# Layer 1 of a two-layer diffusion backbone: query products and the expert blocks computed ahead in plain float32, from weights that are not split

## The chip, the cores and the metric

One Trainium2 chip; the kernel runs on one of its cores. The metric is the device time of one execution in microseconds, lower is better. A core has TensorE (PE; its weight loads are listed as PEld), VectorE (DVE), ScalarE (ACT), GpSimd (POOL) and SyncE (SP), which here issues nearly all DMAs. The kernel keeps its tiles in SBUF on 128 partitions, and its matmuls write to a ring of eight PSUM tiles.

## The reference

Two layers, each a mixer (conv, attention, Hyena and SSD groups between an input and an output projection) and then a PEER expert layer. All is float32. The mixer is the same before and after; the change is in the expert layer:

```python
def peer(h, wq, sub_keys, u_tab, v_tab):          # h: tokens x 1024
    q = (hb @ wq).reshape(128, 8, 2, 128)          # 8 heads, two half queries
    s = einsum('thpk,hpnk->thpn', q, sub_keys)     # scores against 128 keys per half
    v1, i1 = top_k(s[:, :, 0], 16); v2, i2 = top_k(s[:, :, 1], 16)
    cv, ci = top_k(v1[..., :, None] + v2[..., None, :], 16)   # best 16 of the pairs
    e = i1[ci // 16] * 128 + i2[ci % 16]           # expert numbers out of 16,384
    g = softmax(cv)
    act = gelu(einsum('td,ted->te', hb, u_tab[e]))
    return einsum('te,ted->td', g * act, v_tab[e])
```

In layer 1 only the 256 latent tokens go through it (two tiles of 128 tokens); layer 0 has 512 (256 latent, 256 context).

## The kernel before

**Dense experts.** For all but one tile of layer 0 the experts are not gathered. The 16,384 experts are 128 blocks of 128; for each block the kernel computes all activations (`u_stage`: eight k-slices of the block against the token columns `hT`, gelu), multiplies them by a dense gate matrix that is zero except at the chosen experts (`weights`), and multiplies the result with the block of v (`values`, `accum`, into PSUM tiles `ov`).

**Split products.** A float32 product is made of three float32r matmuls (`mm3`, lines 141 to 143). Both operands are first split (`split`, lines 136 to 138): ACT casts to `hi` (line 137), and another engine subtracts to get `lo` (line 138). For the query weights (`load_w`, tile `w_raw`) and the blocks computed ahead that engine is POOL; in the main loop, and for the last four blocks computed ahead, it is DVE.

**Stages of layer 1's expert layer**, in the order of the program:

1. `to_hT` (line 781) transposes the tokens, applies the modulation and splits the result into `hT[0]`, `hT[1]`.
2. For q = 0 to 15, `wq(q)` loads 128 columns of the query weights, splits them and multiplies (tile `pq`, copied to `qs`); `top(q-1)` scores against the keys (tile `ss`, line 1050, two tiles of tokens, plain float32) and takes the best 16 on DVE (lines 1058 to 1062). After every fourth q, `pairs` (lines 1071 to 1135) combines four halves into expert numbers and gates, nearly all on DVE.
3. `u_stage` for blocks 0 to 11, then (`UE`) for 12 to 17.
4. `slots` transposes the routing (`tr`, `slT`); `hots` and `gates` (lines 1182 to 1218) build the gate matrix: for each of 16 groups of 16 tokens DVE makes `Ah`, `Al` (line 1206) and `B_` (line 1209), PE makes 32 float16 matmuls into `G`, ACT copies them to `stg`, and SP writes 1 MB to DRAM (`Gd`). After each group one `u_stage` is issued (blocks 18 to 33); four more follow the last.
5. The main loop runs `u_stage(38)` to `u_stage(127)`, each with the gating and the v-product of a block 38 earlier. It needs the gate matrix read back (`gt`), so the first `ov` matmul of the layer comes after the last `Gd` write.

The tiles of activations (`act`) are 38 (`UA` + `UB`), hence 38 blocks ahead. `u_raw` has three buffers in layer 1 (`URB`), `w_raw` three, and the `hi` and `lo` of a block three each (of the query weights three, `WB`). All loads of `u_raw` are issued after the last load of query weights, on SP's queue, in order with the `Gd` writes. A planner orders the instructions of each engine from its own estimate of their durations; within an engine that order is then fixed.

Of the kernel before, what the change touches and what calls it, by code (L numbers as in the profile page):

```python
# [20 lines left out]
D = 1024  # L21
# [23 lines left out]
NE = 2  # L45
WHB = (4, 5)
WB = 3
FL = 6
FM = 11
LF = 200  # L50
NF = 2
HB = 3
GTB = (4, 4)
GRB = (3, 2)
UEV = (0, 0)
# [28 lines left out]
def tile_hybrid_diffusion(ctx: ExitStack, tc: tile.TileContext, I: dict, out: bass.AP):  # L84
    nc = tc.nc
    V, S, G, T = nc.vector, nc.scalar, nc.gpsimd, nc.tensor
    uid = [0]

    def pool(name, bufs=1, stack=ctx, **k):
        uid[0] += 1  # L90
        if "space" not in k:
            k["reuse_waits"] = "tile"
        return stack.enter_context(tc.tile_pool(name=f"{name}{uid[0]}", bufs=bufs, **k))
# [3 lines left out]
    def mk(p, shape, dt=F32, tag=None, name=None, **k):  # L97
        uid[0] += 1
        n = f"{name or tag}_{uid[0]}"
        if tag in SCR:  # L100
            k["bufs"] = SCR[tag]
        return p.tile(shape, dt, tag=tag or n, name=n, **k)
# [17 lines left out]
    def bank(name="pb"):  # L120
        return mk(ps, [128, 512], F32, tag="b", name=name)
# [12 lines left out]
    late = {}  # L134

    def split(src, hi, lo, eng=None):
        S.copy(hi, src)  # L137
        late["V" if eng in (None, V) else "G"] = (eng or V).tensor_tensor(lo, src, hi.bitcast(F32), ALU.subtract)  # L138

    def mm3(o, lh, ll, rh, rl, first, last):  # L140
        T.matmul(o, lh, rh, start=first, stop=False)  # L141
        T.matmul(o, lh, rl, start=False, stop=False)  # L142
        return T.matmul(o, ll, rh, start=False, stop=last)  # L143
# [97 lines left out]
    def load_w(wp, src, n=128, eng=None, bufs=2, rb=3):  # L241
        raw = mk(wp, [128, 8, 128], tag="w_raw", bufs=rb)
        late["D"] = nc.sync.dma_start(raw[:, :, :n], src)
        hi = mk(wp, [128, 8, 128], F32R, tag="w_hi", bufs=bufs)
        lo = mk(wp, [128, 8, 128], F32R, tag="w_lo", bufs=bufs)
        split(raw[:, :, :n], hi[:, :, :n], lo[:, :, :n], eng or G)
        return hi, lo
# [54 lines left out]
    def ln_mod(l, which, mod, m0):  # L302

        lt = mk(smp, [128, 4, 8], tag="lnT", bufs=2)
        nc.sync.dma_start(lt, I["lnT"][l])
        cc = mk(smp, [128, 2, 8, 2], tag="lnc", bufs=2)
        sc, sh = mod[:, m0 + 8:m0 + 16, :], mod[:, m0:m0 + 8, :]
        for j in range(2):
            V.tensor_tensor(cc[:, j], sc, lt[:, 2 * which + j, :, None].to_broadcast([128, 8, 2]), ALU.mult)
        V.tensor_tensor(cc[:, 1], cc[:, 1], sh, ALU.add)  # L310
        return cc
# [466 lines left out]
        run(ssd(), attention(), hyena(), conf_norm(), more)  # L778
        mp_s.close()

    def to_hT(tiles, xsrc, cc, hT, p, back=None, hb=2):

        for t in tiles:
            s = t // 2
            for q in range(2):
                b = bank("xT")
                for j in range(4):
                    k = 4 * q + j
                    T.transpose(b[:, j * 128:(j + 1) * 128], xsrc(t)[:, k * 128:(k + 1) * 128], ident)
                h = mk(p, [128, 4, 128], tag="h", bufs=hb)  # L790
                for j in range(4):
                    k = 4 * q + j
                    sc, sh = cc[:, 0, k, s:s + 1], cc[:, 1, k, s:s + 1]
                    if j % 2:
                        S.activation(h[:, j, :], b[:, j * 128:(j + 1) * 128], AF.Identity, bias=sh, scale=sc)
                    else:
                        V.tensor_scalar(h[:, j, :], b[:, j * 128:(j + 1) * 128], sc, sh, op0=ALU.mult, op1=ALU.add)
                sl = slice(t * 128, t * 128 + 128)
                split(h, hT[0][:, 4 * q:4 * q + 4, sl], hT[1][:, 4 * q:4 * q + 4, sl])
                if back and t in back:  # L800
                    b = bank("hb")
                    for j in range(4):
                        T.transpose(b[:, j * 128:(j + 1) * 128], h[:, j, :], ident)
                    S.copy(back[t][:, q * 512:q * 512 + 512], b)
# [28 lines left out]
    def fill_to(l, c):  # L833
        while done[-1] < (l, c) and next(fill, None):
            pass
# [7 lines left out]
    for l in range(2):  # L843
        NS = 2 if l == 0 else 1
        NT = 256 * NS
        NTL = 2 * NS
        GT = [3] if l == 0 else []
        DT = [t for t in range(NTL) if t not in GT]
        ND = 128 * len(DT)
        modT = modTs[l]  # L850
        if l == 0:
            hT = [mk(hp, [128, 8, 512], F32R, tag=f"hT{j}") for j in range(2)]

        order = ExitStack()
        with ExitStack() as mx:
            wp = pool("wp", bufs=2, stack=mx)
# [14 lines left out]
            else:  # L871
                with ExitStack() as hs_:
# [40 lines left out]
                    for k in range(0, 8, 2):  # L913
                        for s in range(2):
                            sl = slice(s * 256, s * 256 + 256)
                            h = mk(hmp, [128, 2, 256], tag="h2")
# [29 lines left out]
            if l == 0:  # L946
                xp_s = ExitStack()
                x_n = mk(pool("xp", stack=xp_s, side="right"), [128, 4, D], name="x_n")
# [18 lines left out]
            for m in range(8):  # L967
                wt = load_w(wp, I["w_out"][l, m], eng=V, bufs=WLB[l], rb=WRB[l])
                b = bank("po")
# [3 lines left out]
                for s in range(NS):  # L973
                    sl = slice(s * 256, s * 256 + 256)
# [11 lines left out]
            lnc = ln_mod(l, 0, modT, 24)  # L986
# [12 lines left out]
        hT = [mk(hp, [128, 8, 512], F32R, tag=f"hT{j}") for j in range(2)]  # L999
        if GT:  # L1000
            h2n = mk(rk, [128, D], name="h2n")
# [1 line left out]
        rings = [(up, UA[l])]  # L1003
        gsl = {}

        def u_stage(bl, eng=None):
            raw = mk(up, [128, 8, 128], tag="u_raw", bufs=URB[l])
            with tc.issue_after(late["D"].ins):
                nc.sync.dma_start(raw, I["uT"][l, bl])
            hi = mk(up, [128, 8, 128], F32R, tag="u_hi", bufs=2 + l)  # L1010
            lo = mk(up, [128, 8, 128], F32R, tag="u_lo", bufs=2 + l)
            split(raw, hi, lo, eng)
            b = bank("au")
            for k in range(8):
                mm3(b[:, :ND], hi[:, k, :], lo[:, k, :], hT[0][:, k, :ND], hT[1][:, k, :ND], k == 0, k == 7)
            p, n = rings[0] if bl % (UA[l] + UB[l]) < UA[l] else rings[1]
            a = mk(p, [128, ND], tag="act", bufs=n)
            S.activation(a, b[:, :ND], AF.Gelu_apprx_tanh)
            acts[bl] = a

        with ExitStack() as rt:
            rp = pool("rp", stack=rt)
            sl4 = mk(rp, [128, NTL, 4, 8, 16], name="sl4")
            dec = mk(rp, [128, 3, 16], F16, name="dec")
            nc.sync.dma_start(dec, I["dec"])
            with ExitStack() as wqs:
                wp = pool("wq", bufs=2, stack=wqs)
                rp2 = pool("rp2", bufs=1, stack=wqs)
                if l:
                    prep.clear()  # L1030
                    prep.update(raw=(wp, 2))
                to_hT(range(NTL), lambda t: x_n[:, t, :], lnc, hT, rp2, {3: h2n} if GT else None, HB)
                keys = mk(rp2, [128, 16, 128], tag="keys", bufs=1)
                nc.sync.dma_start(keys, I["keys"][l])
                n8 = 2 * NTL
                vs, ixs, sq = {}, {}, {}

                def wq(q):
                    hi, lo = load_w(wp, I["wq"][l, q], bufs=WB)
                    b = bank("pq")  # L1040
                    for k in range(8):
                        mm3(b[:, :NT], hi[:, k, :], lo[:, k, :], hT[0][:, k, :NT], hT[1][:, k, :NT], k == 0, k == 7)
                    sq[q] = mk(rp2, [128, NT], tag="qs", bufs=2)
                    S.copy(sq[q], b[:, :NT])

# [91 lines left out]
                for q in range(17):  # L1137
# [6 lines left out]
                    if q:  # L1144
                        top(q - 1)
                        if q % 4 == 0:
                            pairs(q // 4 - 1)
                    if done[-1] < (1, (FL, 11)[l]):
                        next(fill)
                fill_to(1, (FL, 11)[l])  # L1150
                ahead = iter(range(min(UA[l] + UB[l], 128)))
                for bl in range(UA[l]):
                    u_stage(next(ahead), G)
            xp_s.close()
            if l == 0:
                fwp_s.close()
# [62 lines left out]

            cur = hots(slots(DT[0]))  # L1220
            for _ in range(UE[l]):
                u_stage(next(ahead), V if UEV[l] else G)
            for i, t in enumerate(DT):
                for tb in range(8):
                    gates(t, tb, *cur)
                    if i + 1 < len(DT):
                        if tb == 2:
                            nxt = slots(DT[i + 1])
                        elif tb == 7:
                            nxt = hots(nxt)  # L1230
                    if tb % 8 in UM[l]:
                        for bl in ahead:
                            u_stage(bl, G)
                            break
                cur = nxt
            for bl in ahead:
                u_stage(bl)


        UBl = UA[l] + UB[l]  # L1240
        with ExitStack() as vst:
# [85 lines left out]
            if l == 0:  # L1327
                lnc = ln_mod(l, 1, modTs[1], 0)
# [16 lines left out]
            for st in range(UBl, last + UBl):  # L1345
                if st < 128:
                    u_stage(st)
                bl = st - UBl
# [17 lines left out]
            x_n = mk(pool("xp", stack=xp_s, side="right"), [128, len(DT), D], name="x_n")  # L1366
# [8 lines left out]
            if l == 0:  # L1375
                hT = [mk(hp, [128, 8, 512], F32R, tag=f"hT{j}") for j in range(2)]
# [152 lines left out]
```

## Time and profile before

| | |
|---|---|
| median of 3 runs | 2943.63 us (2938.61 to 2950.10) |
| profiled execution, time | 2948.22 us |
| profiled execution, span of the core | 2946.4 us |
| mean granted TensorE clock | 0.957 of full speed |
| busy share of the span | PE 90%, PEld 78%, DVE 71%, ACT 40%, POOL 26% |
| share of the chain that ended last | PE 46%, DVE 20%, DMA 14%, issue 12%, POOL 5%, ACT 3% |

Times in the rows are counted from the start of the span. Layer 1's expert layer begins at about 2045. A matmul's duration in the trace includes its way through the array, and matmuls overlap; what one costs in a stream is the distance of two starts. Where rows say x8, eight instructions are merged into one row.

### The profile page before, as it was taken

Reading aid. Unit: us, or ns where it says so; the run is one execution under the profiler, and the core shown is the slowest. Engines: PE = TensorE matmul, PEld = TensorE weight load, DVE = VectorE, ACT = ScalarE, POOL = GpSimd, SP = SyncE. Lnnn points to the kernel's source line nnn. Section 1 sums busy time; section 2 is a strip of 40 time slices with the busy share of each in tenths; the row PEclk is TensorE's granted clock in tenths of the full one; section 3 lists DMA queues with packets and bytes.
Section 4 is the critical chain, followed back from the end, with each engine's and each line's share of the span. In section 5 each row is a group of like instructions: output and inputs, shape, how many; then the busy total and the mean of one; then the engine's idle time right before and its main releaser. Section 6 shows DMA issues by size and latency. Waiting matters only on the chain.

```text
span 2946.4 us, 41926 instructions
## 1 busy us (share of the span) xinstructions
PE 2656.8 (90%) x15646; PEld 2286.7 (78%) x15646; DVE 2099.5 (71%) x4255; ACT 1164.1 (40%) x1810; POOL 778.3 (26%) x505
## 2 busy tenths in 40 slices
PE   6798879688899999999999998788778999999997
PEld 3674557478899988888888987656777999999986
DVE  4956448989687778777767646964999865555556
ACT  2333533235433333333333334334345544444443
POOL 2333013134224444444334103321564100000000
PEclk9899989889899999999999999998888999999999
DMA  7122434336899999988889645325336986666656
GB/s 255 57 90 94 150 122 137 112 117 245 286 334 311 326 321 321 319 307 302 305 308 308 200 129 179 119 82 183 115 116 231 319 272 202 217 209 210 200 181 197
DMA packets 241840, 625.08 MB, mean 212 GB/s; under 512 B 22424, under 2 KB 104794, under 8 KB 236004
## 3 DMA queue, kind: packets, MB, share of 16 engines
q1 hardware_dynamic: 201156, 475.05, 48.6%
q0 software_dynamic: 40480, 147.36, 14.1%
q8 instruction: 122, 2.00, 0.3%
q14 instruction: 82, 0.67, 0.1%
HBM read 573.04 MB, written 49.30 MB: 211 GB/s over the span
## 4 chain that ended last, share of the span: by engine, by line
PE 46%; DVE 20%; DMA 14%; issue 12%; POOL 5%; ACT 3%; SPq 0%; POOLq 0%; DVEq 0%; ACTq 0%
DMA grow<-in_vg_dram,eu 8%; PE ov L142 6%; PE ov L141 6%; PE ov L143 5%; POOL grow L1311 5%; PE au L141 4%; PE au L143 4%; PE au L142 4%; DVE yT L365 2%; PE pj L141 1%; PE pj L142 1%; PE pj L143 1%; DMA wa_raw<-in_w_ada_dram 1%; DVE accg L1324 1%; DVE e L1067 1%
## 5 line engine op out<-in xcount | busy, mean ns | idle before, releaser
L143 PE MATMUL au<-hT,u_lo 128*128 128x384 f32 (+1 forms) x2048 | 642.0, 314 | 12.6 <-POOL u_lo L138 10.0
L141 PE MATMUL au<-hT,u_hi 128*128 128x384 f32 (+1 forms) x2048 | 645.4, 315 | 6.4 <-ACT u_hi L137 3.4
L142 PE MATMUL au<-hT,u_hi 128*128 128x384 f32 (+1 forms) x2048 | 641.5, 313 | 0.0
L142 PE MATMUL ov<-v_lo,wh 128*128 128x512 f32 x1280 | 505.2, 395 | 28.2 <-DVE v_lo L138 27.8
L143 PE MATMUL ov<-v_hi,wl 128*128 128x512 f32 x1280 | 500.1, 391 | 0.0
L141 PE MATMUL ov<-v_hi,wh 128*128 128x512 f32 x1280 | 462.9, 393 | 5.9 <-ACT wh L137 5.6
L137 ACT CAST u_hi<-u_raw 128x1024 fp32r<-128x1024 f32 x256 | 268.7, 1050 | 496.1 <-PE au L142 319.8
L141 PEld LDWEIGHTS au<-hT,u_hi 128*128 128x128 f32 x2048 | 394.1, 192 | 15.3 <-ACT u_hi L137 4.2
L143 PEld LDWEIGHTS au<-hT,u_lo 128*128 128x128 f32 x2048 | 393.2, 192 | 15.6 <-POOL u_lo L138 10.9
L142 PEld LDWEIGHTS au<-hT,u_hi 128*128 128x128 f32 x2048 | 394.1, 192 | 7.7
L138 DVE TENSOR_TENSOR v_lo<-v_raw,v_hi 128x1024 fp32r<-128x1024 f32 x255 | 312.8, 1227 | 79.4 <-ACT v_hi L137 79.1
L138 DVE TENSOR_TENSOR u_lo<-u_raw,u_hi 128x1024 fp32r<-128x1024 f32 x198 | 242.0, 1222 | 148.1 <-ACT u_hi L137 148.1
L137 ACT CAST v_hi<-v_raw 128x1024 fp32r<-128x1024 f32 x256 | 268.3, 1048 | 143.2 <-DMA v_raw<-in_v_dram 109.5
L142 PEld LDWEIGHTS ov<-v_lo,wh 128*128 128x128 f32 x1280 | 241.8, 189 | 84.2 <-DVE v_lo L138 40.9
L137 ACT CAST wh<-act 128x384 fp32r<-128x384 f32 (+1 forms) x256 | 116.9, 459 | 431.1 <-PE ov L142 419.7
L141 PEld LDWEIGHTS ov<-v_hi,wh 128*128 128x128 f32 x1280 | 242.0, 190 | 51.4 <-ACT wh L137 5.9
L143 PEld LDWEIGHTS ov<-v_hi,wl 128*128 128x128 f32 x1280 | 241.5, 189 | 49.7
L138 POOL TENSOR_TENSOR w_lo<-w_raw,w_hi 128x1024 fp32r<-128x1024 f32 (+1 forms) x72 | 176.9, 2466 | 251.5 <-ACT w_hi L137 219.6
L138 POOL TENSOR_TENSOR u_lo<-u_raw,u_hi 128x1024 fp32r<-128x1024 f32 x58 | 171.4, 2961 | 257.3 <-ACT u_hi L137 250.8
L1311 POOL DMA_INDIRECT grow<-in_vg_dram,eu x128 | 179.0, 1398 | 221.5 <-DVE accg L1324 167.2
L1311 POOL DMA_INDIRECT grow<-in_ug_dram,eu x128 | 160.6, 1255 | 262.8 <-DVE grow L1315 232.2
L1324 DVE SCALAR_TENSOR_TENSOR accg<-grow,ag,accg 128x1024 f32<-128x1024 f32 x127 | 162.8, 1282 | 75.8 <-DMA grow<-in_vg_dram,eu 75.1
(832 smaller groups left out, 4324.9 us busy)
## 6 DMA issues: line engine op xcount, KB each, us to landing
u_raw<-in_uT_dram SPq DMA_DIRECT2D x256, 512.0 KB
v_raw<-in_v_dram SPq DMA_DIRECT2D x256, 512.0 KB
Gd<-stg SPq DMA_DIRECT2D x40, 1024.0 KB
gt<-Gd SPq DMA_DIRECT2D x80, 512.0 KB
wa_raw<-in_w_ada_dram SPq DMA_DIRECT2D x76, 512.0 KB
w_raw<-in_w_in_t_dram SPq DMA_DIRECT2D x44, 512.0 KB
w_raw<-in_wq_dram SPq DMA_DIRECT2D x32, 512.0 KB
w_raw<-in_w_ada_dram SPq DMA_DIRECT2D x20, 512.0 KB
```

The source lines that it names most:

```text
L137: S.copy(hi, src)
L138: late["V" if eng in (None, V) else "G"] = (eng or V).tensor_tensor(lo, src, hi.bitcast(F32), ALU.subtract)
L141: T.matmul(o, lh, rh, start=first, stop=False)
L142: T.matmul(o, lh, rl, start=False, stop=False)
L143: return T.matmul(o, ll, rh, start=False, stop=last)
L365: V.scalar_tensor_tensor(uc, upad[:, m, :, j:j + 256], wj, uc, op0=ALU.mult, op1=ALU.add)
L1067: V.tensor_tensor(x[:, :, :, 0:w], x[:, :, :, 0:w], x[:, :, :, w:2 * w], ALU.add)
L1311: nc.gpsimd.indirect_dma_start(out=r, out_offset=None, in_=I[tab], in_offset=bass.IndirectOffsetOnAxis(ap=eu[:, i:i + 1], axis=0))
L1324: V.scalar_tensor_tensor(accg, r, ag[:, i:i + 1], accg, op0=ALU.mult, op1=ALU.add)
```

## The change

Three pairs of switches, all off for layer 0 and on for layer 1. `to_hT` writes its result in float32 into a new tile `h32` and does not split it; the split into `hT` for the main loop is issued inside `wq(1)`. `wq` loads the query weights into five buffers (`PRB`) and multiplies them unsplit with `h32`, one plain float32 product per k-slice. `u_stage` does the same for the 38 blocks computed ahead. The main loop is as before.

```diff
+PW = (0, 1)
+PU = (0, 1)
+PRB = (4, 5)
...
-    def to_hT(tiles, xsrc, cc, hT, p, back=None, hb=2):
+    def to_hT(tiles, xsrc, cc, hT, p, back=None, hb=2, h32=None):
...
-                h = mk(p, [128, 4, 128], tag="h", bufs=hb)
+                h = h32(t)[:, 4 * q:4 * q + 4, :] if h32 else mk(p, [128, 4, 128], tag="h", bufs=hb)
...
-                split(h, hT[0][:, 4 * q:4 * q + 4, sl], hT[1][:, 4 * q:4 * q + 4, sl])
+                if not h32:
+                    split(h, hT[0][:, 4 * q:4 * q + 4, sl], hT[1][:, 4 * q:4 * q + 4, sl])
...
-        def u_stage(bl, eng=None):
+        def u_stage(bl, eng=None, plain=False):
             raw = mk(up, [128, 8, 128], tag="u_raw", bufs=URB[l])
             with tc.issue_after(late["D"].ins):
                 nc.sync.dma_start(raw, I["uT"][l, bl])
+            if plain:
+                b = bank("au")
+                for k in range(8):
+                    T.matmul(b[:, :ND], raw[:, k, :], h32[0][:, k, :ND], start=k == 0, stop=k == 7)
+                return act_of(bl, b)
...
                 def wq(q):
-                    hi, lo = load_w(wp, I["wq"][l, q], bufs=WB)
                     b = bank("pq")
-                    for k in range(8):
-                        mm3(b[:, :NT], hi[:, k, :], lo[:, k, :], hT[0][:, k, :NT], hT[1][:, k, :NT], k == 0, k == 7)
+                    if PW[l]:
+                        raw = mk(wp, [128, 8, 128], tag="w_raw", bufs=PRB[l])
+                        late["D"] = nc.sync.dma_start(raw, I["wq"][l, q])
+                        o = 0
+                        for h in h32:
+                            n = h.shape[-1]
+                            for k in range(8):
+                                T.matmul(b[:, o:o + n], raw[:, k, :], h[:, k, :], start=k == 0, stop=k == 7)
+                            o += n
+                        if q == 1:
+                            for i in range(0, 8, 2):
+                                split(h32[0][:, i:i + 2, :], hT[0][:, i:i + 2, :ND], hT[1][:, i:i + 2, :ND])
...
-                    u_stage(next(ahead), G)
+                    u_stage(next(ahead), G, PU[l])
...
-                u_stage(next(ahead), V if UEV[l] else G)
+                u_stage(next(ahead), V if UEV[l] else G, PU[l])
...
-                            u_stage(bl, G)
+                            u_stage(bl, G, PU[l])
...
-                u_stage(bl)
+                u_stage(bl, None, PU[l])
```

## Rows read from the trace of the kernel before

**Rows 1.** Busy by stretch: length, PE, PEld, DVE, ACT, POOL, clock, DMA, GB/s.

```profile
2323.00:2900.00 577.00, 575.87 (x3535) 518.15 (x3535) 353.03 (x572) 278.90 (x416) 6.79 (x9) 1.00 0.69 222
2052.00:2323.00 271.00, 218.62 (x1904) 212.88 (x1904) 240.50 (x628) 126.72 (x215) 125.32 (x48) 0.89 0.53 177
2063.00:2192.00 129.00, 97.94 (x713) 95.38 (x712) 124.31 (x543) 54.61 (x87) 69.24 (x28) 0.87 0.35 112
2222.00:2307.00 85.00, 73.67 (x826) 71.33 (x824) 81.02 (x49) 50.37 (x92) 35.91 (x13) 0.96 0.76 261
```

**Rows 2.** POOL's groups, 2040 to 2310.

```profile
L138 POOL TENSOR_TENSOR u_lo<-u_raw,u_hi 128x1024 fp32r<-128x1024 f32 x34 | 91.6, 2702 | 89.9 <-ACT u_hi L137 85.9 <-PE au L142 2.2 <-PE G L1216 1.8
L138 POOL TENSOR_TENSOR w_lo<-w_raw,w_hi 128x1024 fp32r<-128x1024 f32 x16 | 39.3, 2464 | 31.8 <-ACT w_hi L137 31.7
```

**Rows 3.** DVE in order of time: start, duration, line.

```profile
2076.93 2.53 DVE L1083 TENSOR_TENSOR cand<-v 128x8 f32<-128x8 f32 x3
...
2113.33 2.11 DVE L1133 TENSOR_SCALAR rb<-rb 128x64 f32<-128x64 f32 x1
...
2172.06 0.20 DVE L1133 TENSOR_SCALAR rb<-rb 128x64 f32<-128x64 f32 x1
...
2182.72 2.67 DVE L1067 TENSOR_TENSOR e<-e 128x128 f16<-128x128 f16 x2
...
2226.48 1.21 DVE L1206 TENSOR_TENSOR Ah<-o,o 128x2048 f16<-128x2048 f16 x1
```

**Rows 4.** DVE's costliest groups, 2192 to 2306.

```profile
L1206 DVE TENSOR_TENSOR Al<-o,o 128x2048 f16<-128x2048 f16 x16 | 30.4, 1902 | 0.0
L1206 DVE TENSOR_TENSOR Ah<-o,o 128x2048 f16<-128x2048 f16 x16 | 29.4, 1843 | 4.7 <-PE G L1215 4.7
```

**Rows 5.** PE in order of time, at three places.

```profile
2602.00 0.28 PE L141 MATMUL au<-hT,u_hi 128*128 128x256 f32 x1
2602.12 0.28 PE L142 MATMUL au<-hT,u_hi 128*128 128x256 f32 x1
...
86.04 1.89 PE L238 MATMUL kf<-h4a,dft 128*128 128x256 f32 x8
...
2115.24 0.61 PE L1050 MATMUL ss<-keys,qs 128*128 128x128 f32 x4
```

**Rows 6.** Plain float32 products: count, least/median/longest duration, first and last start.

```profile
L238 PE MATMUL kf<-h4a,dft x32: 377/379/379, 86.0 to 179.1; 128*128 128x256 f32 x32
...
L1050 PE MATMUL ss<-keys,qs x64: 272/275/583, 2062.6 to 2133.3; 128*128 128x128 f32 x64
```

**Rows 7.** Layer 1's tokens, queries and blocks ahead: tiles xT, qs, au.

```profile
L795 ACT ACTIVATE h<-xT,lnc x8: 451/457/476, 2047.4 to 2055.6; 128x128 f32<-128x128 f32 x8
...
L1044 ACT COPY qs<-pq x16: 359/367/392, 2062.2 to 2132.4; 128x256 f32<-128x256 f32 x16
...
L141 PE MATMUL au<-hT,u_hi x312: 278/283/563, 2133.3 to 2322.6; 128*128 128x256 f32 x156
```

**Rows 8.** The gate stage and the first v-product: tiles G, stg, ov.

```profile
L1215 PE MATMUL G<-Ah,B__3321_18911 x16: 218/218/233, 2221.5 to 2223.2; 128*128 128x128 f16 x16
...
L1217 ACT ACTIVATE stg<-G x64: 587/602/677, 2219.7 to 2306.6; 128x512 f32<-128x512 f32 x64
...
L141 PE MATMUL ov<-v_hi,wh x512: 388/389/497, 2323.4 to 2930.7; 128*128 128x512 f32 x171
```

**Rows 9.** PE's longest waits, 2052 to 2320: total, times, longest.

```profile
PE ss L1050 <- ACT qs L1044: 16.9, 5, 8.3
PE G L1215 <- DVE Ah L1206: 12.1, 2, 7.5
```

**Rows 10.** A block's load: issue on SP, and its cast on ACT.

```profile
2139.94 3.24 SPq L1009 DMA_DIRECT2D u_raw<-in_uT_dram  x2
...
2143.89 1.04 ACT L137 CAST u_hi<-u_raw 128x1024 fp32r<-128x1024 f32 x1
```

**Rows 11.** The page's group of a split on DVE.

```profile
L138 DVE TENSOR_TENSOR u_lo<-u_raw,u_hi 128x1024 fp32r<-128x1024 f32 x198 | 242.0, 1222 | 148.1 <-ACT u_hi L137 148.1
```

More of the change, by code (lines that the diff above doesn't have):

```diff
@@ L1015, in u_stage, with act_of @@
                 mm3(b[:, :ND], hi[:, k, :], lo[:, k, :], hT[0][:, k, :ND], hT[1][:, k, :ND], k == 0, k == 7)
+            act_of(bl, b)
+        def act_of(bl, b):
             p, n = rings[0] if bl % (UA[l] + UB[l]) < UA[l] else rings[1]
@@ L1024, in tile_hybrid_diffusion @@
             dec = mk(rp, [128, 3, 16], F16, name="dec")
+            h32 = []
+            if PW[l]:
+                h32.append(mk(rp, [128, 8, ND], name="h32"))
             nc.sync.dma_start(dec, I["dec"])
@@ L1031, in tile_hybrid_diffusion, with cols32 @@
                     prep.update(raw=(wp, 2))
-                to_hT(range(NTL), lambda t: x_n[:, t, :], lnc, hT, rp2, {3: h2n} if GT else None, HB)
+                if PW[l] and GT:
+                    h32.append(mk(rp2, [128, 8, 128], name="h32g"))
+                def cols32(t):
+                    return h32[1] if t in GT else h32[0][:, :, t * 128:(t + 1) * 128]
+                to_hT(range(NTL), lambda t: x_n[:, t, :], lnc, hT, rp2, {3: h2n} if GT else None, HB, cols32 if PW[l] else None)
                 keys = mk(rp2, [128, 16, 128], tag="keys", bufs=1)
@@ L1038, in wq @@
                 def wq(q):
-                    hi, lo = load_w(wp, I["wq"][l, q], bufs=WB)
                     b = bank("pq")
-                    for k in range(8):
-                        mm3(b[:, :NT], hi[:, k, :], lo[:, k, :], hT[0][:, k, :NT], hT[1][:, k, :NT], k == 0, k == 7)
+                    if PW[l]:
+                        raw = mk(wp, [128, 8, 128], tag="w_raw", bufs=PRB[l])
[9 more added lines that the diff above has]
+                                split(h32[0][:, i:i + 2, :], hT[0][:, i:i + 2, :ND], hT[1][:, i:i + 2, :ND])
+                    else:
+                        hi, lo = load_w(wp, I["wq"][l, q], bufs=WB)
+                        for k in range(8):
+                            mm3(b[:, :NT], hi[:, k, :], lo[:, k, :], hT[0][:, k, :NT], hT[1][:, k, :NT], k == 0, k == 7)
                     sq[q] = mk(rp2, [128, NT], tag="qs", bufs=2)
```

## The prediction, made before the changed kernel was run

> **What bounds the kernel now.** I read busy time by stretch first. In the main loop, 2323 to 2900, PE is busy for 575.87 of 577 us [rows 1]: that stretch is PE's work and the change does not touch it. So the change is worth what it moves the first v-product, at 2323.4 [rows 8]. Ahead of that, from 2052, PE is busy for 218.62 of 271 us at a granted clock of 0.89, while DVE is busy for 240.50 and, while the experts are chosen, for 124.31 of 129 [rows 1]. The chain of waits, read in order of time, agrees: between the first scores and the last gates it is made almost wholly of DVE pieces.
>
> Then I asked why DVE is so busy. Read in order of time, the same operation on the same shape takes 2.11 us in one place and 0.20 in another [rows 3], and each long one lies beside one of POOL's subtractions, of which there are 16 of 2.46 us and 34 of 2.70 [rows 2]. From 2063 to 2192 I count 23 such stretched rows, the first and the last of them in [rows 3], about 1.8 us over their like: 41 us. In the gate stage `Al` and `Ah` take 1.90 and 1.84 us on average against 1.21 undisturbed [rows 3, 4]: 16 x 0.69 + 16 x 0.63 = 21 us, and other operations of that stage wait too.
>
> PE's longest waits in this part are for scores and gates that hang on DVE [rows 9].
>
> **The change part by part.**
>
> *POOL's 50 subtractions go,* and with them 54 casts of ACT and the four subtractions of the last blocks ahead, which DVE did. Nothing of POOL's is left in this part. Value for DVE: 41 us while the experts are chosen and at least 21 at the gates. Its ends: nothing, if the stretched operations wait for something else, and all of it.
>
> *Each product of three float32r matmuls becomes a plain float32 one.* Three float32r matmuls of 256 columns cost 3 x 0.12 us (starts 2602.00 and 2602.12 [rows 5]), so 8 k-slices cost 2.88. For plain float32 the row is `kf`: eight instructions of 256 columns in 1.89, of which the last's own way through is 0.38 [rows 5, 6], so (1.89 - 0.38) / 7 = 0.216 each. The trap is the count. Layer 1's scores are 16 x 2 = 32 products in the code, and the trace has 64 [rows 6]; `kf` is 16 products in the code, and the trace has 32. A plain product is two instructions, 0.43 us, and a block is 16 x 0.216 = 3.46 us. So PE gets slower: 16 query products and 38 blocks, 54 x (3.46 - 2.88) = 31 us more work. The switch that saves the splits costs TensorE.
>
> The Trainium skill has two sentences on this. "FP8 and Floating Point Precision", section "TensorE Precision Notes", says that true FP32 takes four passes through the array; "Perfetto Trace Analysis", section "Engine Utilization", halves the output rate for FP32_LOW_HIGH. The trace sides with the four: each instruction takes somewhat under twice a float32r one's time, and there are two. By the second alone a block would be 1.73 us; that is rival 3.
>
> *`to_hT` no longer splits; the split is inside `wq(1)`.* The tokens are ready at about 2051 instead of 2055.6 [rows 7], as four subtractions of DVE no longer stand between them. The same four, with four casts, come after `pq(1)`: some 0.6 us each on DVE, half of a block's 1.22 [rows 11], 2.5 in all. They lie in DVE's wait for the first scores, since PE now needs 3.46 + 0.4 us a query (four score instructions, (0.61 - 0.28) / 3 = 0.11 each [rows 5, 6]) and DVE some 2.4; without that cover they cost 2.5 us of DVE. The first result on DVE moves little, to about 2062.
>
> *Five buffers of query weights, three of blocks.* A load now holds its buffer until PE has multiplied. A block's load was issued at 2139.94 and its cast began at 2143.89 [rows 10], so about 4 us; with three buffers a block can follow every (4 + 0.5 + 3.46) / 3 = 2.7 us, less than the 3.46 that PE takes. SP's queue holds the `Gd` writes and the loads in order; in the gate stage a round moves 1 MB + 0.5 MB. At PE's pace, below, that is 1.57 MB in 5.3 us, 296 GB/s, against 261 at a DMA share of 0.76 [rows 1], so a share of 0.86. I charge a few us for loads that come late there; bounds 0 and, if the DMA share can't go above 0.76, 16 x 0.7 = 11 us.
>
> *What is late next: PE.* Its work from the first query product to the first v-product, at full clock: queries 16 x 3.46 = 55; scores 64 x 0.11 = 7; 38 blocks x 3.46 = 131; 16 groups of 32 gate matmuls, sixteen of them 1.7 us apart [rows 8], so 1.85 a group, 30; block 38 of the main loop 2.9; transposes 1. Together 227 us; before it was 196, which took 271 with 23 lost to a lower clock (196 / 0.89 is the 219 of busy time) and 52 waiting.
>
> DVE no longer limits it. From 2062 it has 83 us of choosing left (124 - 41) and 2.5 of splits, so the routing is ready near 2150, where it was 2192; PE, queries and scores behind it at 2051 + 62 + some 5, is then in blocks 0 to 17 (18 x 3.46 = 62 us, to about 2180), and the first gates can be built under them. In the gate stage PE needs 1.85 + 3.46 = 5.3 us a group, DVE 3 x 1.21 = 3.6 [rows 3], ACT 4 x 0.6 and a gelu. The pace before was (2306.6 - 2219.7) / 15.75 = 5.5, so the stage hardly gains; the gain is that it starts earlier.
>
> The sum: first v-product at 2051 + 227 = 2278 with no waiting and full clock, a gain of 45 at most. I take 17 us of the former 75 as staying: some 4 for a slow first product, 5 for heads of queue while DVE sets the pace of the scores, 4 for late loads, 4 for clock after gaps. Gain 2323 - 2295 = 28 us. From the profiled execution's 2948.2 that is 2920; its median is 4.6 below that execution, so 2943.6 - 28 = 2916.
>
> **The rivals.**
>
> 1. *No change.* The gaps of PE stay because they come from order (blocks behind the last query product, the transposes behind DVE), not from the stretched operations. If 44 of the 75 us stay, the 31 us of extra work eat the gain. For it: order on PE is fixed, and 16.9 us of waits hang on ACT's copies. Against it: those copies wait for DVE. Time about 2942.
>
> 2. *Slower: PE is the bound and its clock does not rise.* PE waits as before, because each query now takes 3.9 us, and scores reach DVE later by what DVE saves; the extra work then runs at 0.89 beside the same 52 us of waiting: 227 / 0.89 + 52 = 307 us against 271, so +36 at the worst and about +15 if a third of the waits goes: 2959. It decides once more than 271 - 255 = 16 us of waiting stays at that clock. For it: the clock is 0.87 while the experts are chosen. Against: it is 1.00 where PE is never idle, and 0.96 in the gate stage [rows 1], and PE will be idle less.
>
> 3. *A plain product costs one instruction's time.* Then a block takes 1.73, PE's work falls to 227 - 54 x 1.73 = 134, and DVE sets the pace: routing at 2148, first gates copied 15 us later, 15.75 groups at the DMA's pace of 4.6 us (1.57 MB at 261 / 0.76 = 343 GB/s), then 17 to the first v-product as before (2323.4 - 2306.6): 2252, gain 71, so 2873. The counts in rows 6 speak against it.
>
> 4. *Transfers.* The gate stage falls to the DMA share of before and pays the 11 us above, with loads late in the blocks before it too: gain 15, 2929.
>
> **How the numbers follow.** My forecast (with its own spread from 2900 to 2926) gets 0.63, rival 1 0.13, rival 2 0.08, rival 3 0.04, rival 4 0.12. A measurement of this kernel tells 0.5%, about 15 us, from no change, so faster means below 2929. Faster: the forecast, rival 3 and most of rival 4, 0.75. Same: rival 1 and the rest of 4, 0.17. Slower 0.08. The low end is the 45 us of PE's full-clock floor, 2898; the high end takes in rivals 4 and 1, 2941; rivals 2 and 3 stay out.
>
> **What the changed profile would show.** POOL idle from 2046 to the main loop, and no DVE operation of lines 1067 to 1135 over 1 us. A block ahead as 16 instructions 0.216 apart. The routing ready near 2150, DVE no longer full after it. PE busy for over 225 us between the first query product and the first v-product, at a clock above 0.93, with `ov` first near 2295. Wrong would be: eight instructions a block; stretched DVE operations with POOL idle; gates more than 6 us apart; or a main loop that is not 623 us from the first `ov` to the end.

## The result, and the profile after

The changed kernel takes 2911.9 us (median of 4 runs, 2903.46 to 2918.5), the kernel before beside it 2945.79: a ratio of 0.9886 (95% interval 0.9852 to 0.992), so 34 us faster. The forecast was 2916. The profiled execution took 2903.46 us, its span is 2901.5 and its mean granted clock 0.962.

First the busy time by stretch of layer 1's expert layer (columns as in [rows 1]): the main loop; from the first query product to the first v-product; the choosing of experts; the rest of the blocks ahead of the gates; the gate stage; and the tail behind the gates.

```profile
2277.40:2870.00 592.60, 591.81 (x3599) 531.73 (x3600) 359.68 (x578) 283.84 (x422) 6.81 (x9) 1.00 0.72 220
2038.60:2277.40 238.80, 230.11 (x1474) 205.02 (x1473) 159.19 (x633) 84.63 (x173) 0.00 (x0) 0.99 0.60 199
2047.00:2136.00 89.00, 87.15 (x425) 77.08 (x424) 83.16 (x544) 28.44 (x54) 0.00 (x0) 0.98 0.41 130
2136.00:2168.00 32.00, 32.00 (x154) 28.09 (x153) 11.12 (x12) 4.11 (x11) 0.00 (x0) 1.00 0.50 149
2168.00:2250.00 82.00, 82.00 (x754) 74.42 (x752) 53.07 (x47) 38.60 (x80) 0.00 (x0) 1.00 0.81 290
2250.00:2277.40 27.40, 20.59 (x112) 18.32 (x109) 7.89 (x23) 8.35 (x17) 0.00 (x0) 0.93 0.78 249
```

POOL is empty up to the main loop, PE is full from the choosing to the last gate, and its granted clock from the first query product to the first v-product is 0.99, where it was 0.89 in [rows 1]. The same two views as [rows 3] and [rows 4]: DVE in order of time, then its two groups of the gate stage.

```profile
2067.05 0.20 DVE L1133 TENSOR_TENSOR gw<-tv 128x64 f32<-128x64 f32 x1
...
2097.04 0.31 DVE L1116 TENSOR_TENSOR cand<-v 128x8 f32<-128x8 f32 x3
...
2103.22 0.17 DVE L1166 TENSOR_SCALAR rb<-rb 128x64 f32<-128x64 f32 x1
```

```profile
L1239 DVE TENSOR_TENSOR Ah<-o,o 128x2048 f16<-128x2048 f16 x14 | 17.1, 1225 | 31.1 <-PE G L1248 31.1
L1239 DVE TENSOR_TENSOR Al<-o,o 128x2048 f16<-128x2048 f16 x14 | 17.1, 1218 | 0.0
```

The `cand` row of three took 2.53 us before and takes 0.31; `rb` took up to 2.11 and takes 0.17; `Ah` and `Al` fall from 1.84 and 1.90 to 1.22. `Ah` now waits 31.1 us for PE: the roles have changed. The instructions of the plain products, two rounds of gates, and the first v-product (count, least/median/longest duration, first and last start), as in [rows 6 to 8]:

```profile
L1067 PE MATMUL pq<-h,w_raw x256: 379/379/483, 2038.6 to 2100.3; 128*128 128x256 f32 x128
L1017 PE MATMUL au<-h,u_raw x608: 379/379/634, 2104.1 to 2267.3; 128*128 128x256 f32 x152
L1248 PE MATMUL G<-Ah,B__3331_18652 x16: 218/218/219, 2211.0 to 2212.7; 128*128 128x128 f16 x16
L1248 PE MATMUL G<-Ah,B__3342_18713 x16: 218/218/219, 2216.3 to 2218.0; 128*128 128x128 f16 x16
L1250 ACT ACTIVATE stg<-G x64: 590/602/616, 2168.5 to 2250.5; 128x512 f32<-128x512 f32 x64
L144 PE MATMUL ov<-v_hi,wh x512: 388/389/796, 2277.4 to 2885.9; 128*128 128x512 f32 x171
```

256 instructions are 16 x 8 products twice, 608 are 38 x 8 twice. In order of time, 48 of them take 10.52 us, so (10.52 - 0.38) / 47 = 0.216 each:

```profile
2109.80 10.52 PE L1017 MATMUL au<-h,u_raw 128*128 128x256 f32 x48
```

PE's waits of 2038 to 2300, against [rows 9], are only two, and the one of 6.8 us is new. SP's queue in the tail (start, duration until SP goes on, issues) shows where it comes from, and SP's longest wait of 2245 to 2285 behind it says what SP stands on:

```profile
PE ov L144 <- ACT v_hi L140: 6.8, 1, 6.8
PE ss L1083 <- ACT qs L1077: 1.8, 1, 1.8
```

```profile
2253.90 13.21 SPq L1013 DMA_DIRECT2D u_raw<-in_uT_dram  x5
2267.16 1.05 SPq L1282 DMA_DIRECT2D gt<-Gd  x2
2268.26 3.54 SPq L1294 DMA_DIRECT2D v_raw<-in_v_dram  x3
```

```profile
SPq L1013 <- PE au L1017: 13.8, 5, 3.0
```

SP stands 13.21 us on five loads of `u_raw`, since the buffers are held until PE has multiplied the plain blocks, up to the last; only then come the gate matrix and the first v.

### The profile page after: what moved, and what is told of

The parts are those of the page before. It is cut to its first block, busy times and chain, and to the rows that moved or that the text cites. A ratio compares the mean times of both kernels' runs of the same rounds, so it can differ in the third digit from the quotient of the medians.

```text
span 2901.5 us, 40897 instructions
## 1 busy us (share of the span) xinstructions
PE 2674.6 (92%) x15214; PEld 2281.7 (79%) x15214; DVE 2011.8 (69%) x4251; ACT 1114.9 (38%) x1756; POOL 645.4 (22%) x455
## 4 chain that ended last, share of the span: by engine, by line
PE 52%; DVE 15%; DMA 13%; issue 11%; POOL 6%; ACT 2%; SPq 0%; POOLq 0%; DVEq 0%; ACTq 0%
DMA grow<-in_vg_dram,eu 7%; PE ov L145 5%; PE ov L144 5%; PE ov L146 5%; POOL grow L1344 5%; PE au L146 4%; PE au L144 4%; PE au L1017 4%; PE au L145 4%; DVE yT L368 2%; PE pj L144 1%; PE pj L145 1%; PE pj L146 1%; DMA grow<-in_lnr_dram 1%; DMA wa_raw<-in_w_ada_dram 1%
## 5 line engine op out<-in xcount | busy, mean ns | idle before, releaser
L146 PE MATMUL au<-hT,u_lo 128*128 128x384 f32 (+1 forms) x1744 | 552.2, 317 | 10.1 <-POOL u_lo L141 6.8
L144 PE MATMUL au<-hT,u_hi 128*128 128x384 f32 (+1 forms) x1744 | 553.2, 317 | 3.0 <-DVE slT L1212 3.0
L145 PE MATMUL au<-hT,u_hi 128*128 128x384 f32 (+1 forms) x1744 | 551.2, 316 | 0.0
L140 ACT CAST u_hi<-u_raw 128x1024 fp32r<-128x1024 f32 x218 | 228.9, 1050 | 460.4 <-PE au L145 321.4
L146 PEld LDWEIGHTS au<-hT,u_lo 128*128 128x128 f32 x1744 | 331.2, 190 | 13.3 <-POOL u_lo L141 7.4
L144 PEld LDWEIGHTS au<-hT,u_hi 128*128 128x128 f32 x1744 | 331.7, 190 | 11.0 <-DVE slT L1212 3.4
L145 PEld LDWEIGHTS au<-hT,u_hi 128*128 128x128 f32 x1744 | 331.5, 190 | 7.7
L1348 DVE SCALAR_TENSOR_TENSOR grow<-grow,h2n 128x1024 f32<-128x1024 f32 x128 | 155.9, 1222 | 61.4 <-DMA grow<-in_ug_dram,eu 59.6
L141 DVE TENSOR_TENSOR wl<-act,wh 128x384 fp32r<-128x384 f32 (+1 forms) x256 | 125.3, 491 | 96.8 <-ACT wh L140 96.2
```

The source lines that it names most:

```text
L1348: V.scalar_tensor_tensor(r, r, 1.0, h2n, op0=ALU.mult, op1=ALU.mult, accum_out=ag[:, i:i + 1])
```

## The experiments

Each ran beside the kernel before, whose medians were 2945.8 to 2947.7. A profile shows one execution of each. The table counts the landmarks of each profile from layer 1's first token transpose: the first query product, the routing ready (the last `sl`), the first gate matmul, the first v-product, the end.

| kernel | us | ratio, interval | query | routing | gates | v | end |
|---|---|---|---|---|---|---|---|
| before | 2945.8 | | 6.8 | 146.6 | 168.8 | 277.7 | 900.8 |
| the change | 2911.9 | 0.9886, 0.9852 to 0.992 | 3.3 | 100.7 | 132.6 | 242.1 | 866.2 |
| again | 2910.7 | 0.9875, 0.9855 to 0.9894 | 3.4 | 100.7 | 132.6 | 241.7 | 865.7 |
| pool_back | 2935.4 | 0.9948, 0.9927 to 0.997 | 3.5 | 132.1 | 156.1 | 265.4 | 890.7 |
| pool_write | 2955.3 | 1.0032, 1.0013 to 1.0051 | 35.9 | 134.7 | 164.9 | 274.5 | 900.5 |
| act_back | 2918.3 | 0.9905, 0.9878 to 0.9931 | 3.3 | 103.4 | 134.8 | 243.9 | 869.7 |
| query_only | 2925.4 | 0.993, 0.9906 to 0.9954 | 3.3 | 123.3 | 144.7 | 254.5 | 876.4 |
| blocks_only | 2923.8 | 0.9923, 0.9896 to 0.995 | 7.6 | 121.1 | 142.1 | 251.5 | 876.4 |
| half_k | 2860.4 | 0.9717, 0.9689 to 0.9744 | 3.5 | 93.1 | 106.4 | 190.5 | 813.8 |
| sub_dve | 2908.0 | 0.9867, 0.9847 to 0.9888 | 8.2 | 132.9 | 149.3 | 242.9 | 865.9 |
| gt_first | 2913.0 | 0.9887, 0.986 to 0.9914 | 3.3 | 100.7 | 130.9 | 238.7 | 866.4 |
| hybrid | 2902.3 | 0.985, 0.9827 to 0.9872 | 3.5 | 102.0 | 132.2 | 224.6 | 848.0 |
| hybrid2 | 2891.6 | 0.9814, 0.9792 to 0.9836 | 3.3 | 101.9 | 129.5 | 224.4 | 848.9 |
| both_layers | 2903.6 | 0.9854, 0.9823 to 0.9885 | 3.5 | 102.0 | 132.2 | 241.7 | 866.7 |

**again**, no edit. 

> The changed kernel once more, unchanged. In the first profile the layer 1 part, from the first query product to the first v-product, was 32 us shorter than before (270.9 to 238.8), and layer 0's part, which the change does not touch, was some 9 us shorter too. Theory A (the 9 us are the spread of one execution): the profile here shows the 239 us again within 3, layer 0's part anywhere within 10 us of before, and the time is 30 to 38 us below before. Theory B (the change reaches layer 0 through the planner's order): layer 0's part is 9 us shorter again and the time is 40 us or more below.

In the first profile layer 1 began at 2035.3, 10 us earlier than before; here it begins at 2044.4 (before: 2045.7) with layer 1 the same. So those 10 us are layer 0's spread; the gain lies between the first transpose and the first v-product, 277.7 to 242.

**pool_back**: POOL's subtractions alone, 54 of them, as the last four blocks ahead have one here too. 

> The changed kernel, with POOL subtracting every query weight and every block computed ahead from itself into a tile that nothing reads: POOL's 54 operations are back, PE's, ACT's and the loads' work is as after the change. Theory A (POOL's operations stretch DVE's, and their absence is the gain): DVE operations of 2 us and more are back beside POOL's, the routing is ready some 30 to 40 us later than after the change, gates come at 5.6 to 5.9 us a group, and the time is that of before within 8 us, about 2940. Rival (the gain comes from ACT's casts, the loads or the tokens ready sooner): the time stays within 5 us of the changed kernel's 2912.

```diff
             if plain:
+                lo = mk(up, [128, 8, 128], F32R, tag="u_lo", bufs=2 + l)
+                G.tensor_tensor(lo, raw, raw, ALU.subtract)
...
```

(and likewise for `w_raw`). 24.7 us of the gain are lost (against the repeated run), and the routing is 31 us later, on a result that nobody reads. From the first scores to the routing DVE is busy for 114 us again, where the change had 83:

```profile
2057.00:2177.20 120.20, 103.39 (x479) 89.29 (x478) 113.99 (x544) 29.12 (x59) 51.00 (x26) 0.92 0.38 115
```

POOL and DVE in order of time:

```profile
2079.76 1.89 POOL L1066 TENSOR_TENSOR w_lo<-w_raw 128x1024 fp32r<-128x1024 f32 x1 [1.96 <-DMA w_raw<-in_wq_dram]
2079.95 0.20 DVE L1129 FIND_INDEX8 tix<-tv,cand 128x8 uint32<-128x50 f32 x1
2080.07 1.67 DVE L1137 TENSOR_TENSOR gw<-tv 128x64 f32<-128x64 f32 x1
...
2083.75 1.89 POOL L1066 TENSOR_TENSOR w_lo<-w_raw 128x1024 fp32r<-128x1024 f32 x1 [2.10 <-DMA w_raw<-in_wq_dram]
2083.90 1.83 DVE L1142 TENSOR_TENSOR sl<-gw,gz 128x64 f32<-128x64 f32 x1
2085.65 0.68 DVE L1153 TENSOR_TENSOR e<-e,dec 128x1024 f16<-128x1024 f16 x1
...
2087.45 1.89 POOL L1066 TENSOR_TENSOR w_lo<-w_raw 128x1024 fp32r<-128x1024 f32 x1 [1.81 <-DMA w_raw<-in_wq_dram]
2087.87 1.75 DVE L1104 TENSOR_TENSOR e<-e 128x512 f16<-128x512 f16 x1
```

Each of these held DVE instructions ends 0.1 to 0.3 us behind POOL's (2081.74 and 2081.65; 2085.73 and 2085.64; 2089.62 and 2089.34): it sits there until POOL is done, and then does its own work. `gw`, which takes 1.67 here, takes 0.20 after the change. `FIND_INDEX8`, beside POOL too, takes its usual 0.20. The larger instructions of the gate stage show the same, and that it goes both ways:

```profile
2231.41 1.21 DVE L1243 TENSOR_TENSOR Al<-o,o 128x2048 f16<-128x2048 f16 x1
2232.05 2.32 POOL L1016 TENSOR_TENSOR u_lo<-u_raw 128x1024 fp32r<-128x1024 f32 x1 [2.78 <-DMA u_raw<-in_uT_dram]
2232.55 2.91 DVE L1246 TENSOR_TENSOR B__3357_18665<-iE,slT 128x2048 f16<-128x2048 f16 x1
```

POOL starts while `Al` runs and ends 1.75 us behind it (2234.37 and 2232.62), about what a subtraction takes by itself (1.89); `B_` starts while POOL runs and ends 1.1 us behind it (2235.46), about what it takes by itself (1.21).

My expectation missed twice. The time stayed 12 us below before, where I had allowed 8; by the rows a subtraction is shorter here than in the kernel before (last section). And the gates stayed 5.34 apart, not 5.6 to 5.9, since there PE, not DVE, sets the pace, and the holding falls into DVE's wait.

**pool_write**: the same, POOL filling tiles in place of subtracting. 

> The changed kernel, with 50 fills by GpSimd in the places of its 50 subtractions: each fills a tile of [128,8,128] that nothing reads with zeros, so GpSimd writes as many bytes as a subtraction wrote but reads none. Theory A (what stretches VectorE's short instructions is GpSimd's reading and writing of two operands; an instruction that only writes is shorter or holds VectorE less): 2908 to 2918 us, routing ready under 110 us behind the first transpose. Rival (any GpSimd instruction of that size stretches VectorE): as the run with the subtractions put back, 2928 to 2940, routing ready 125 to 135, VectorE's small copies near 2 us again beside a fill.

```diff
-                G.tensor_tensor(lo, raw, raw, ALU.subtract)
+                G.memset(lo.bitcast(F32), 0.0)
...
```

(an edit against pool_back, in both places). Neither theory saw this. A fill needs no input, so all ran at once, ahead of the queries. POOL's fills of 2051 to 2090 as groups, the one DVE instruction that these met, and the same instruction in the changed kernel and in pool_back:

```profile
L1016 POOL MEMSET u_lo<- 128x1024 f32 x28 | 25.4, 951 | 0.0
L1066 POOL MEMSET w_lo<- 128x1024 f32 x12 | 11.1, 951 | 0.0
```

```profile
2051.76 35.34 DVE L994 TENSOR_SCALAR x_n<-x_n,ln_rs 128x1024 f32<-128x1024 f32 x1 [9.97 <-POOL ln_rs L302]
```

```profile
2033.97 0.81 DVE L994 TENSOR_SCALAR x_n<-x_n,ln_rs 128x1024 f32<-128x1024 f32 x1 [1.24 <-POOL ln_rs L302]
```

```profile
2043.58 2.36 DVE L994 TENSOR_SCALAR x_n<-x_n,ln_rs 128x1024 f32<-128x1024 f32 x1 [1.23 <-POOL ln_rs L302]
```

A 0.81 us instruction took 35.34: it waited for the whole train, whose last fill ends at 2086.55, and ended at 2087.10. In pool_back it met two subtractions back to back (from 2043.50 and from 2045.35) and took 2.36: it came in behind the first, and the second ended 1.75 us behind it. So fills keep it out for the whole train, and subtractions do not; why they differ, no run shows. From the first query on the layer is the changed kernel's (274.5 - 35.9 = 238.6, against 238.8), so the train is nearly the whole price: 32.6 us there and 8.7 more of waiting for `ln_rs` behind the fills (9.97 - 1.24), 41 of 44 in all. That POOL's reading is needed to hold DVE is refuted for this instruction; the fills met no `TENSOR_TENSOR`, so whether they hold one, and what spaced fills would cost among the choosing, stays open.

**act_back**: ACT's casts alone, 54 as in the kernel before. 

> The changed kernel, with ScalarE's 50 casts of layer 1 put back: each raw plain weight tile of [128,8,128] is copied to a tile that nothing reads (about 1.9 us each, some 95 us of ScalarE in all); the products stay plain and GpSimd does nothing. Theory A (what the change gave back beside TensorE came from GpSimd's subtractions, not from ScalarE's casts, and ScalarE has room): within 6 us of the changed kernel, 2906 to 2918 us; routing ready 98 to 106 us behind the layer's first transpose, first v-product 238 to 246 behind it, GELU-gate groups still 5.3 us. Rival (the casts held the layer as well, through the tokens that ScalarE copies between the products): 2922 us or more, routing ready over 110.

```diff
+                hi = mk(up, [128, 8, 128], F32R, tag="u_hi", bufs=2 + l)
+                S.copy(hi, raw)
...
```

(and likewise for `w_raw`). The time, 2918.3, is at the edge of theory A's range, its interval overlaps with the changed kernel's, and the landmarks from the routing on move by 1.8 to 4 us. The casts (1.05 us each, not the 1.9 I had written) cost a few us, by the medians at most 8.

**query_only** and **blocks_only**: one half of the change each. 

> Only the query products are plain; the 38 blocks are split as before. Theory A: 16 of POOL's 50 subtractions are gone, all of them from the part in which the experts are chosen: 16 x 1.8 = 29 us less for DVE there and 4 us from the tokens being ready sooner, against subtractions of blocks that now fall earlier into this part; gates at 5.5 us a group as before. Time 2920 to 2928, a gain of 18 to 26. If the blocks alone make the gain (rival): under 8 us.

> Only the 38 blocks computed ahead are plain; the query weights are split as before and the tokens are split before the first query product (and kept in float32 beside it). Theory A: DVE keeps 16 stretched operations while the experts are chosen, the last query product comes some 15 us later than after the change, and from there PE is the bound as after the change: 18 blocks of 3.46 us, gates at 5.33 us a group. Time 2925 to 2933, a gain of 13 to 20. Rival (the query products alone make the gain, PE's slower blocks cost what POOL's absence gives): no gain, within 5 us of before.

```diff
-PU = (0, 1)
+PU = (0, 0)
```

That is query_only; blocks_only sets `PW = (0, 0)` in its place, splits the tokens ahead of the queries and keeps them in float32 for the blocks. They gain 22 and 24 us (blocks_only some 1 us better than its range), 46 together, where both give 34 to 37. Each takes part of POOL's work away while PE still has waits to absorb the longer products (30 us of waits in query_only and 22 in blocks_only from the first query product to the first v-product); with both, 8.6 us are left.

**half_k**: is PE the bound now? 

> The changed kernel with every other k-slice left out of the plain products (queries and the 38 blocks ahead), so that each costs PE 1.73 us instead of 3.46; all else as after the change. It leaves out half of those sums. Theory A (PE is the bound from the first query product to the first v-product): PE's work there falls from 227 to 134 us, DVE and the loads set the pace, gates come at 4.5 to 5 us a group, and the time falls to 2870 to 2890. Rival (DVE or the loads bound that part already): within 8 us of the changed kernel's 2911.

```diff
-                for k in range(8):
+                for k in range(0, 8, 2):
...
```

(in the blocks and the queries alike). Half of the plain products is 54 x 1.73 = 93 us of PE, and 51 came out at the end: PE was the bound, until others take over. The gain is larger than I expected. Its longest waits:

```profile
PE tr L1208 <- DVE sl L1168: 22.5, 1, 22.5
PE au L1017 <- DMA u_raw<-in_uT_dram: 6.0, 8, 2.4
```

**sub_dve**: the kernel before, with its layer 1 subtractions on DVE and the products still split. 

> The kernel before, with layer 1's subtractions of query weights and blocks ahead done by DVE (1.22 us each) instead of POOL. All products split, PE's work as before. POOL does nothing there, so no DVE operation is stretched, but DVE has 50 x 1.22 = 61 us more of its own against some 80 us of stretching. Theory A: while the experts are chosen about even (41 against 34 x 1.22 = 41), gates at 4.8 to 5 us a group instead of 5.5; time 2930 to 2942, a gain of 6 to 18. Rival (POOL's absence alone is the gain, whoever subtracts): the changed kernel's 2911.

```diff
-UEV = (0, 0)
+UEV = (0, 1)
...
-                    hi, lo = load_w(wp, I["wq"][l, q], bufs=WB)
+                    hi, lo = load_w(wp, I["wq"][l, q], eng=V if l else None, bufs=WB)
...
-                    u_stage(next(ahead), G)
+                    u_stage(next(ahead), V if l else G)
...
-                            u_stage(bl, G)
+                            u_stage(bl, V if l else G)
```

My expectation fell, its rival held: the whole gain of the change without one plain product. DVE carries 50 subtractions more (1.22 us each, [rows 11]) and is done sooner than before, since none of its instructions is held any more: from the first query product to the first v-product it is busy for 213 us, where [rows 1] had 240 without that work. The limit is another one, though. The whole stretch, then choosing and gates, and PE's longest wait:

```profile
2048.30:2283.00 234.70, 201.69 (x1905) 199.38 (x1906) 213.16 (x677) 126.46 (x215) 0.00 (x0) 0.92 0.59 204
2058.80:2173.00 114.20, 83.50 (x689) 82.94 (x689) 112.82 (x571) 53.12 (x83) 0.00 (x0) 0.87 0.41 130
2189.40:2265.60 76.20, 74.29 (x879) 73.27 (x877) 73.37 (x67) 51.73 (x96) 0.00 (x0) 1.00 0.87 317
```

```profile
PE tr L1175 <- DVE sl L1135: 29.8, 1, 29.8
```

While the experts are chosen DVE is full (112.82 of 114.2) and PE is not; in the gate stage the 16 rounds take 76 us, where the changed kernel's plain blocks take 82.

**gt_first**: the tail's wait of 6.8 us taken away by the order on SP. 

> The changed kernel, with the first reads of the gate matrix issued on SP before the loads of the main loop's first blocks; after the change they were issued behind a load that waits for the last plain block, and PE then stood still for 6.8 us before the first v-product. Theory A (that wait comes from the order on SP): the wait falls to 1 us or less, time 2903 to 2907. Rival (the wait is for the transfers themselves, which run at 334 GB/s there): no change, 2909 to 2912.

```diff
...
+                        if l and bl == 0:
+                            late["D"] = ld
...
```

(`ld` is the read of `gt`, and the loads of the main loop's `u_raw` are issued behind it; the gating of block 0 goes ahead of the main loop's first block for that). The theory failed; 2913.0 is the changed kernel's time. The first v-product comes 3 us sooner (238.7), the end does not (866.4); the wait has moved to the main loop's first block:

```profile
PE au L144 <- ACT u_hi L140: 7.0, 1, 7.0
```

**hybrid** and **hybrid2**: plain where DVE is full, split on DVE where PE is full. In hybrid the queries and blocks 0 to 17 are plain, the other 20 blocks split; in hybrid2 only the queries and blocks 0 to 7 are plain. 

> The changed kernel, but the 16 blocks of the gate stage and the 4 after it are split again, the subtraction on DVE; queries and blocks 0 to 17 stay plain. Theory A (in the gate stage PE is the bound at 5.33 us a group while DVE has 1.7 us a group to spare): PE needs 1.85 + 2.88 = 4.73 us a group, DVE 3.6 + 1.22 = 4.8; with the four blocks behind it 10 us less: 2898 to 2906. Rival (the transfers of the stage, 1.57 MB a group, bound it): 0 to 4 us less, 2907 to 2911.

> As the mixed kernel (2902 us), but only the queries and expert blocks 0 to 7 in plain float32; blocks 8 to 17 are split too, by VectorE (a subtraction of 1.2 us and ScalarE's cast of 1.9 us each). By the rows: ten blocks fewer in plain float32 save TensorE 10 x 0.58 = 6 us, and cost VectorE 10 x 1.2 = 12 us in the stretch in which the tokens are chosen, where VectorE had some 15% free. Theory A (TensorE and VectorE are both near full there, so that the time stands still): 2897 to 2906 us. Rival (VectorE becomes the bound, as in the kernel that splits all on VectorE): 2906 to 2912 us, routing ready over 112 us behind the first transpose.

```diff
-                            u_stage(bl, G, PU[l])
+                            u_stage(bl, V if l else G)
...
```

hybrid hits its range, and hybrid2 with 2891.6 is some 5 below its own. Choosing and gates by stretch, hybrid first:

```profile
2047.50:2147.80 100.30, 98.42 (x480) 86.80 (x479) 88.40 (x555) 34.92 (x70) 0.00 (x0) 0.98 0.40 127
2178.00:2253.00 75.00, 73.97 (x878) 73.17 (x876) 70.88 (x64) 52.63 (x97) 0.00 (x0) 1.00 0.92 328
```

```profile
2040.00:2140.10 100.10, 94.95 (x461) 83.37 (x460) 89.39 (x557) 36.50 (x71) 0.00 (x0) 0.98 0.38 121
2167.70:2245.20 77.50, 76.94 (x900) 75.88 (x899) 73.85 (x67) 52.54 (x96) 0.00 (x0) 1.00 0.87 307
```

Both keep the changed kernel's routing (102) and the faster gates; the first v-product comes 17 us sooner than with the change. In hybrid some 7 of these are in the gates and the other 10 in the tail (17.3 us against 27.4), where PE's wait of 6.8 us is gone. In these profiles the two do not differ behind it (848.0 and 848.9), and they ran on different chips with intervals that touch, so that hybrid2 is the faster one is not shown. That hybrid2 beats the change is shown by the times; hybrid's interval still overlaps with the change's, and for it the profiles speak (848.0 against 866.2 and 865.7).

**both_layers**: layer 0 too. 

> The changed kernel, with layer 0's queries and ahead-computed expert blocks in plain float32 too. Layer 0's products are wider (query products of 512 columns, blocks of 384), so TensorE pays more for each, while GpSimd's subtractions go there too. Estimate from layer 1's rows, scaled by columns: 16 query products' slices x 8 x about 0.2 us = 26 us and 26 blocks x 8 x about 0.11 = 23 us, some 50 us of TensorE, against up to 40 us of stretched VectorE work. Theory A (TensorE bounds layer 0 as it does layer 1 after the change): 2905 to 2940 us, not faster than the changed kernel by more than 5. Rival (GpSimd's subtractions bound layer 0 as they did layer 1): 2870 to 2900 us.

```diff
-PW = (0, 1)
-PU = (0, 1)
+PW = (1, 1)
+PU = (1, 1)
```

2903.6 is 1.4 us below theory A's range and 7 to 8 below the changed kernel, where I had allowed 5; but the interval overlaps with the changed kernel's. By stretch in layer 0 (400 to 600, 600 to 650, 650 to 775), the changed kernel and then this one:

```profile
400.00:600.00 200.00, 163.93 (x864) 117.14 (x868) 164.41 (x899) 67.04 (x99) 46.02 (x21) 0.86 0.45 143
600.00:650.00 50.00, 40.81 (x231) 38.27 (x224) 44.32 (x82) 17.25 (x22) 20.62 (x7) 0.89 0.25 76
650.00:775.00 125.00, 108.24 (x1088) 103.89 (x1088) 105.70 (x77) 68.00 (x126) 56.19 (x15) 0.97 0.68 245
```

```profile
400.00:600.00 200.00, 176.00 (x1000) 117.22 (x1000) 163.01 (x953) 53.04 (x80) 0.43 (x2) 0.93 0.44 144
600.00:650.00 50.00, 49.24 (x152) 29.79 (x153) 16.48 (x22) 6.51 (x13) 0.00 (x0) 0.93 0.28 85
650.00:775.00 125.00, 125.00 (x1024) 90.90 (x1023) 84.44 (x76) 57.23 (x116) 3.03 (x3) 1.00 0.72 267
```

PE is full from 600 on; from its first transpose to its first v-product layer 0 takes 395.8 us, against 399.6 and, in the repeated run, 396.1. There the exchange is about even.

## Why the prediction was right

**POOL's subtractions hold DVE.** Right, and the heart of it. DVE's busy time while the experts are chosen was to fall from 124 to 83 us; it is 83.16. pool_back brings 31 of these 41 us back (113.99) by adding POOL's work alone, and sub_dve gets the gain by taking only that work off POOL. What I took as "stretched" is an instruction that waits for POOL to finish.

**A plain product costs two instructions of 0.216 us.** Right: 608 and 256 instructions, 0.216 apart, so rival 3 falls.

**PE becomes the bound.** Right: full from 2136 to 2250, rounds 5.3 apart (2211.0 to 2216.3), and half_k turns less PE work into time. PE is near full earlier than I had it, while the experts are chosen (87.15 of 89 us, beside DVE's 83.16). From the first query product I had the routing 99 us later, the end of the 18 blocks 129 and the first v-product 244; measured 97.4, 129.3 (the first gate matmul) and 238.8.

**The clock rises.** 0.99 after 0.89, so rival 2 falls: PE does not idle between its pieces any more. (Its price for a third of the waits gone, "about +15", should be +19 by its own terms, 227 / 0.89 + 35 against 271; nothing else hangs on it.) Rival 1 falls with it.

**Transfers.** The gate stage ran at 290 GB/s and a DMA share of 0.81 without a wait of PE for a load; I had 296 and 0.86. Rival 4's ceiling of 0.76 was none: hybrid reached 0.92 at 328.

**What was off in size.** (1) The residual over 227 us of PE work: 17 charged, 11.8 measured. Heads of queue cost 1.8, not 5; the clock (0.01 of 239) 2.4, not 4; the slow first product nothing that shows; late loads 6.8, not 4, and not in the gate stage, where I had put them, but in the tail behind SP's loads; 0.8 us no row names. (2) The first query product came 3.5 us earlier after the transpose, not 1.5. Together 7 us: in the profiles the first v-product comes 35.6 us sooner (277.7 and 242.1) where I had 28. That the time is within 4 us of the forecast is in part luck, since single executions lie up to 15 us apart. (3) "The gate stage hardly gains": its copies now span 82.0 us (2168.5 to 2250.5), against 86.9 in [rows 8], 4.9 less where the paces gave 3. (4) "The first result on DVE moves little, to about 2062", 16.3 us behind the transpose, was wrong: it comes after 11.7 (2046.95). The routing gained little by that, since DVE then waits for the next queries' scores (1.5 us for each of the next two).

**What the prediction did not ask** is whether the plain products were needed for the gain. They were not: sub_dve has it without them. The change pays 31 us of PE to relieve DVE of something that DVE could do itself in about 61 us (50 x 1.22), once nothing holds it.

## What to carry to other kernels

Where short DVE instructions take 2 us in one place and 0.2 in another, lay POOL's rows beside them before counting DVE as full: work moved to POOL can cost DVE more than it takes off it (240 us of DVE before, 213 with the work moved back), and moving it back is the first thing to try. An exchange of one engine's work for another's pays by stage: here plain products pay while DVE is the bound and cost while PE is, and the mix beat both. Gains of two halves need not add: here each half used waits of PE that the two together had to share.

## What was not expected of the hardware

- One DVE instruction of 0.81 us took 35.34 while POOL ran its fills back to back, 0.951 us each. The Trainium skill, "SBUF — State Buffer", section "Who interferes with whom", says that the engine that comes second is blocked for the whole of the other's instruction and gets no share. The rows of pool_back agree: each held instruction shown above ends 0.1 to 1.1 us behind POOL's, less than it takes by itself, and this same instruction waited for one subtraction alone (2.36). By that sentence alone the fills should cost one fill at most, under 1 us; the trace shows a wait through the whole train, and the measurement decides.
- Which DVE instructions are held is seen in the rows: `TENSOR_TENSOR` on float32 and float16 and `TENSOR_SCALAR` on float32, with all operands in SBUF, are; `FIND_INDEX8` beside the same subtraction is not, and neither is a `TENSOR_SCALAR` that reads a PSUM tile (`xT`). In pool_back it takes its usual 0.41 beside a subtraction of 2047.65 to 2049.54:

```profile
2048.58 0.41 DVE L800 TENSOR_SCALAR h<-xT,lnc 128x128 f32<-128x128 f32 x1
```

- POOL's own subtraction takes 1.89 us in pool_back, with one input tile read twice, and 2.4 in the kernel before, with two, when it starts beside no DVE instruction that holds it:

```profile
2070.51 2.40 POOL L138 TENSOR_TENSOR w_lo<-w_raw,w_hi 128x1024 fp32r<-128x1024 f32 x1 [0.85 <-ACT w_hi L137]
```

  So reading a second tile costs 0.5 us. What [rows 2] have above that on average (2.46 and 2.70) is POOL waiting for DVE: the longer ones start while a DVE instruction runs, and nearly all of these end 2.2 to 2.3 us behind it.
